# First stage of a two-layer attention and convolution trunk: layer 1's modulation columns computed with the modulation weights as stationary fp32 operand

## The chip, the cores and the metric

The kernel runs on one core of a Trainium2 chip. The metric is device time of one execution in microseconds (us); the time before is the median of three runs. A core has a matrix engine (PE, with its weight loads shown as PEld), a vector engine (DVE), a scalar engine (ACT), GpSimd (POOL), and a sync engine (SP) whose queue issues nearly all transfers. Each engine works through its own instruction queue in order and waits there on semaphores of the others.

## The reference

A trunk of two layers on 1024 latent tokens of width 1024 with 256 context tokens: layer 1 is windowed attention that also reads the context, layer 2 a convolution module. Only what feeds layer 1's input projection matters here:

```
silu_c = jax.nn.silu(c)
silu_cc = jax.nn.silu(c_ctx)
...
shift, scale, gate = jnp.split((silu_c @ ada_w[i] + ada_b[i])[:, None, :], 3, axis=-1)
h_lat = modulate(rmsnorm(x, norm_g[i]), shift, scale)
...
shift_c, scale_c, gate_c = jnp.split(silu_cc @ ada_w[i] + ada_b[i], 3, axis=-1)
h_ctx = modulate(rmsnorm(h_ctx_stream, norm_g[i]), shift_c, scale_c)
```

`modulate(h, shift, scale)` is `h * (1 + scale) + shift`. So for layer 1 two vectors (the condition c and the context's c_ctx, 1024 numbers each) are multiplied with the first 2048 columns of `ada_w[0]` (1024 x 3072, fp32; 8 MB of it are read here), and the results scale and shift the 1024 features of the normalised tokens, which are then multiplied with `attn_w_in`.

## The kernel before

Features lie on the 128 partitions, so the 1024 features are 8 tiles, numbered kt. Large products are in a three-term form: each fp32 operand is split into a high part (hh, whi: rounded to the fast fp32r format) and a low part (hl, wlo: the rest), and `mm3` multiplies whi with hh, whi with hl and wlo with hh. An fp32r matmul is one record in the trace.

**The first stage** (lines 310 to 548) makes the modulated, transposed tiles of x and multiplies them with the first three 128-column chunks of `attn_w_in` (key head 0, query head 0, value head 0), accumulated over kt in PSUM as `acc0`. Latent tokens are treated in two halves of 512: half 0 in this stage, half 1 in the loop from line 1071 on, after the results of half 0 (`finished0`) and the context's keys (`ctx0`).

- `ada_load(pr)` (280): loads for a pair of tiles (256 columns of shift and 256 of scale) four pages `araw` of 0.5 MB, each by two transfers with runs of 1 KB, and two short rows of `ada_b`.
- `ada_split` (386): splits each page into `ahi` (ACT) and `alo` (DVE).
- `ada_mm` (397): 16 fp32r matmuls per pair. The condition is the stationary operand, four columns (`c4`: high and low part of two vectors); 512 modulation columns are moving. The result is four rows in PSUM, copied to `R` (trace name arow).
- `ada_cols` (413): turns the rows into columns and adds high, low and bias parts: four fp32 matmuls per pair with the 5-row page of `R` as stationary operand and `sel` (two columns) moving. DVE then writes the shift and the gain, (1 + scale) times the norm weight, to `mods`.
- `sums`, `rstd_of`, `normalise` (339 to 360): row sums of squares, their reciprocal roots, scaling of the token rows. `sums` on ACT is a square (trace name junk) and a short accumulator read.
- `turn` (426): four PE transposes of the row pages give one tile with 512 tokens in PSUM. `x_tile` (432) and `modulated` (371): ACT writes hh from PSUM with gain and shift, DVE writes the full-precision value hf, then DVE or POOL writes hl = hf - hh. `c_tile` (442) does it for the context's 256 tokens.
- `x_mm` (453): three products for each listed weight chunk.
- `wsA.load` and `wsA.split` (212, 221): loads a chunk of `attn_w_in` (0.5 MB, runs of 512 bytes) and splits it on ACT and DVE.
- `spin` (306): products of zeros that nothing reads, placed between waits.

**Order.** A framework schedules instructions that are not pinned by a modelled time; `pin` names the engines whose instructions stay in program order from there on (P, V, A, G, S). PE and DVE are pinned throughout the stage, ACT only up to `pin("PV")` (504); SP is never pinned. Instructions of an unpinned engine can be moved ahead of pinned ones. In the loop over pairs (508) the next pair's `ada_mm` stands ahead of this pair's products, and tiles 0 and 1 of half 1 are turned in its last round (524, 536). All instructions are issued through one helper, so the trace gives the same line, L89, for all of them, and groups are told apart by tile names.

## Time and profile before

| | us |
|---|---|
| median of 3 runs (1755.21 to 1758.65) | 1755.38 |
| span of the profiled execution, first to last instruction | 1752.9 |
| PE busy | 1720.7 (98%) |
| PE weight loads busy | 1424.8 (81%) |
| DVE busy | 1148.3 (66%) |
| ACT busy | 889.4 (51%) |
| POOL busy | 895.4 (51%) |
| share of PE in the chain of work that ended last | 86% |

The mean granted PE clock over the span is 0.996. Records of PE overlap, since matmuls are pipelined: a lone duration is longer than the distance from one start to the next, and it is the distance that counts in a row of them. In the timeline a row is: start, duration, engine, line, operation, out<-in, shape, count, and in brackets how long the engine was idle before and what released it. In groups the two numbers behind the bar are total busy time and mean duration in nanoseconds.

### The profile page before, as it was taken

To read this page: it belongs to the slowest core of one execution; us is meant where nothing else is said; L and a number is where in the kernel's file an instruction comes from. 1 tells how busy PE (TensorE), PEld (TensorE's weight loads), DVE (VectorE), ACT (ScalarE), POOL (GpSimd) and SP (SyncE) were. 2 spreads that over 40 slices of the span, in tenths; PEclk is the share of its full clock that TensorE was granted. 3 is DMA by queue.
4 is the path that set the end of the run, shared out by engine and by line. 5 is a ranking of instruction groups with operands and counts; after the bars stand their busy time and mean duration, and the time that the engine had idled before them with its cause. 6 is when DMAs were issued, how large, how long until landed. Compare 5 with 4: busy or idle time off the path is not lost.

```text
span 1752.9 us, 23877 instructions
## 1 busy us (share of the span) xinstructions
PE 1720.7 (98%) x8420; PEld 1424.8 (81%) x8420; DVE 1148.3 (66%) x2079; ACT 889.4 (51%) x1548; POOL 895.4 (51%) x705
## 2 busy tenths in 40 slices
PE   7999999999999999999999999999999999999997
PEld 4788888888888888888888888888888888788886
DVE  6755564556546563656315189999999999867823
ACT  7555553445345444545334355554665564466731
POOL 0245654566636565653101267998898888130300
PEclk9999999999999999999999999999999999999999
DMA  9334443444334542436777733011121202377971
GB/s 313 107 82 139 136 133 85 145 147 145 100 105 143 152 142 87 136 119 203 279 250 239 241 90 105 13 54 31 43 79 36 91 30 79 120 254 243 325 264 48
DMA packets 195324, 242.45 MB, mean 138 GB/s; under 512 B 11798, under 2 KB 126790, under 8 KB 195204
## 3 DMA queue, kind: packets, MB, share of 16 engines
q1 hardware_dynamic: 188516, 230.10, 40.3%
q10 hardware_dynamic: 6688, 10.83, 2.6%
q8 instruction: 66, 1.08, 0.3%
q14 instruction: 54, 0.44, 0.1%
HBM read 188.70 MB, written 41.69 MB: 131 GB/s over the span
## 4 chain that ended last, share of the span: by engine, by line
PE 86%; DMA 5%; DVE 3%; POOL 2%; ACT 2%; issue 2%; SPq 1%; ACTq 0%; POOLq 0%; DVEq 0%
PE psg L89 44%; PE pss L89 22%; PE pso L89 19%; DMA araw_page<-in_ada_w_dram 1%; POOL rope_half L89 1%; DMA low_page<-in_conv_w_out_dram 1%; DMA rope_half<-rope_half 1%; SPq L89 1%; DMA low_page<-in_attn_w_out_dram 1%; DMA wolC<-low_page 1%; DVE mask_page L89 1%; ACT p_page L89 0%; POOL wlo_page L89 0%; POOL low_page L89 0%; DMA wraw_page<-in_attn_w_in_dram 0%
## 5 line engine op out<-in xcount | busy, mean ns | idle before, releaser
L89 POOL TENSOR_TENSOR odd_half<-odd_half,prod_half 128x513 f32<-128x513 f32 (+2 forms) x252 | 312.8, 1250 | 24.2 <-ACT prod_half L89 11.0
L89 PE MATMUL psg<-hh_page,whi_page 128*128 128x512 f32 x600 | 237.6, 396 | 0.0
L89 PE MATMUL psg<-hh_page,wlo_page 128*128 128x512 f32 x600 | 236.9, 395 | 0.0
L89 PE MATMUL psg<-hl_page,whi_page 128*128 128x512 f32 x600 | 236.8, 395 | 0.0
L89 POOL TENSOR_TENSOR wlo_page<-wraw_page,whi_page 128x1024 fp32r<-128x1024 f32 x70 | 173.1, 2475 | 104.1 <-ACT whi_page L89 83.2
L89 ACT ACTIVATE prod_half<-ubuf,dww 128x513 f32<-128x513 f32 (+2 forms) x252 | 165.1, 674 | 107.3 <-POOL odd_half L89 105.1
L89 POOL TENSOR_SCALAR p_page<-p_page,sc 128x640 f32<-128x640 f32 (+1 forms) x128 | 100.8, 787 | 224.4 <-DVE sc L89 208.7
L89 PE MATMUL psg<-h2h_page,whi_page 128*128 128x512 f32 x464 | 183.9, 396 | 0.0
L89 PE MATMUL psg<-h2h_page,wlo_page 128*128 128x512 f32 x464 | 183.0, 394 | 0.0
L89 PE MATMUL psg<-h2l_page,whi_page 128*128 128x512 f32 x464 | 182.4, 393 | 0.0
L89 DVE SCALAR_TENSOR_TENSOR pss<-ubuf,dww,pss 128x512 f32<-128x512 f32 (+3 forms) x270 | 172.3, 670 | 0.1
L89 DVE SCALAR_TENSOR_TENSOR pss<-ubuf,wsum,pss 128x512 f32<-128x512 f32 (+3 forms) x270 | 171.7, 670 | 0.2
L89 DVE TENSOR_TENSOR ptlo<-pss,pthi 128x640 fp32r<-128x640 f32 (+1 forms) x144 | 103.3, 717 | 64.0 <-ACT pthi L89 62.8
L89 ACT ACTIVATE p_page<-p_page,sc 128x641 f32<-128x641 f32 (+1 forms) x128 | 102.7, 802 | 74.1 <-DVE sc L89 69.7
L89 ACT ACTIVATE pthi<-pss 128x640 fp32r<-128x640 f32 (+1 forms) x144 | 88.6, 615 | 91.7 <-PE pss L89 86.3
L89 PEld LDWEIGHTS psg<-hh_page,wlo_page 128*128 128x128 f32 x600 | 112.9, 188 | 26.3
L89 PEld LDWEIGHTS psg<-hh_page,whi_page 128*128 128x128 f32 x600 | 113.0, 188 | 20.8 <-DVE kvc_page L89 0.2
L89 PEld LDWEIGHTS psg<-hl_page,whi_page 128*128 128x128 f32 x600 | 112.9, 188 | 20.7
L89 ACT ACTIVATE whi_page<-wraw_page 128x1024 fp32r<-128x1024 f32 x88 | 92.6, 1053 | 69.0 <-PE psg L89 25.5
L89 PE MATMUL pso<-h2l_page,whi_page 128*128 128x512 f32 x304 | 119.9, 394 | 0.0
L89 PE MATMUL pso<-h2h_page,whi_page 128*128 128x512 f32 x304 | 119.8, 394 | 0.0
L89 PE MATMUL pso<-h2h_page,wlo_page 128*128 128x512 f32 x304 | 119.6, 394 | 0.0
(244 smaller groups left out, 4105.2 us busy)
## 6 DMA issues: line engine op xcount, KB each, us to landing
wraw_page<-in_conv_w_in_dram SPq DMA_DIRECT2D x48, 512.0 KB
wraw_page<-in_attn_w_in_dram SPq DMA_DIRECT2D x40, 512.0 KB
wol_page<-wolA SPq DMA_DIRECT2D x32, 512.0 KB
wo_page<-in_attn_w_out_dram SPq DMA_DIRECT2D x32, 512.0 KB
wo_page<-in_conv_w_out_dram SPq DMA_DIRECT2D x32, 512.0 KB
wol_page<-wolC SPq DMA_DIRECT2D x32, 512.0 KB
rope_half<-rope_half ACTq DMA_DIRECT2D x80, 128.0 KB
araw_page<-in_ada_w_dram SPq DMA_DIRECT2D x32, 256.0 KB
```

The costliest lines, as they stand in the source:

```text
L89: r = f(*a, **k)
```

## The change

The modulation weights become the stationary operand. For tile kt and j (0 shift, 1 scale) `ada(kt)` multiplies eight 128x128 fp32 blocks of `ada_w`, unsplit, with two moving columns, the fp32 condition `c2`; the result is columns on the partitions at once. Bias and norm weight come in as per-partition scalars: the first 2048 elements of `ada_b` are loaded as 16 more rows of `crow` and transposed with it into `ab0`. `ada_split`, `ada_mm`, `ada_cols`, `c4`, `cf`, `R` and `sel` go.

Loads are per tile: `ada_load(kt)` brings two pages of 0.5 MB with runs of 512 bytes (tiles 0 to 3); `ada_load(4, 2)` and `ada_load(6, 2)` bring two tiles in four pages with runs of 1 KB. The first rows of x are now loaded ahead of all modulation weights, the context's rows after tile 5's weights.

The order of work is rewritten: for tiles 0, 1 and 2 `ada`, `turn`, `x_tile`, the split of one chunk, spins (30, 3, 3, 4 and 5 of them) and the products that are possible; then a loop in which each round has one `ada`, one `x_tile` and the products of the tile before. Context tiles are made two in a round from round 5 on. Tiles 0 and 1 of half 1 are turned after `ctx0("k", 0)`. The sums of squares of x's first half are shared by ACT and DVE, and all low parts of half 0 are made on DVE.

```diff
-ADA_FP = ()
 FILL = 12
+SPIN0 = 30
+SPIN1 = 3
 DEFER = 6
...
     vt = ctile([P, P], F32, "vt")
-    sel = ctile([P, 2], F32, "sel")
+    ab0 = ctile([P, 16], F32, "ab0")
     sink = ctile([P, NH], F32, "sink")
...
     crow_pg = hp.alloc(F32, None, "crow")
-    crow = crow_pg[0:32, 0:P]
+    crow = crow_pg[0:48, 0:P]
     SY.dma_start(out=crow[0:8], in_=c.rearrange("o (r p) -> (o r) p", p=P))
...
     SY.dma_start(out=crow[16:32], in_=norm_g.rearrange("l (r p) -> (l r) p", p=P))
+    SY.dma_start(out=crow[32:48], in_=ada_b[0:1, 0:2048].rearrange("o (r p) -> (o r) p", p=P))
     G.memset(ones, 1.0)
...
-    NPR = KT // 2
-    R = {}
     araw = {}
-    def ada_load(pr):
-        R[pr] = hp.alloc(F32, None, "arow")
-        araw[pr] = [pg.alloc(F32, [2, 2, 256], "araw") for _ in range(4)]
-        for i in range(4):
-            for j in range(2):
-                SY.dma_start(out=araw[pr][i][:, :, j],
-                             in_=ada_w[0, i * 256:i * 256 + 256, j * D + pr * 256:j * D + pr * 256 + 256]
+    def ada_load(kt, n=1):
+        w = n * P
+        for j in range(2):
+            for i in range(n):
+                t = pg.alloc(F32, [KT // n, w], "araw")
+                for m in range(n):
+                    araw[(kt + m, j)] = araw.get((kt + m, j), []) + [(t, slice(m * P, m * P + P))]
+                SY.dma_start(out=t, in_=ada_w[0, i * D // n:(i + 1) * D // n, j * D + kt * P:j * D + kt * P + w]
                              .rearrange("(k p) n -> p k n", p=P))
-        for j in range(2):
-            SY.dma_start(out=R[pr][4:5, j * 256:j * 256 + 256], in_=ada_b[0:1, j * D + pr * 256:j * D + pr * 256 + 256])
...
     spin(4)
+    xs0 = load_rows(x[0, 0:512], 4)
     ada_load(0)
-    xs0 = load_rows(x[0, 0:512], 4)
     wsA.load()
...
     wsA.load()
+    ada_load(2)
     wsA.load()
-    ada_load(2)
...
     tp = ps_g()
-    PE.transpose(tp[:, 0:32], crow, ident[0:32, 0:32])
+    PE.transpose(tp[:, 0:48], crow, ident[0:48, 0:48])
     act(cs, tp[:, 0:16], AF.Silu)
     V.tensor_copy(vt[:, 96:112], tp[:, 16:32])
+    V.tensor_copy(ab0[:, 0:8], tp[:, 32:40])
+    V.tensor_scalar(out=ab0[:, 8:16], in0=tp[:, 40:48], scalar1=1.0, scalar2=None, op0=ALU.add)
     hp.free(crow_pg)
-    ada_load(3)
-    cx = load_rows(ctx[0], 2)
     act(small([P, 1], name="warm", bufs=1), cs[:, 0:1], AF.Sqrt, scale=0.0)
...
     hp.free(zer_pg)
-    c4 = ctile([P, KT, 4], F32R, "c4")
-    csv = cs.rearrange("p (r k) -> p k r", r=2)
-    V.tensor_copy(c4[:, :, 0:2], csv)
-    tt(V, c4[:, :, 2:4], csv, c4[:, :, 0:2].bitcast(F32), ALU.subtract)
+    c2 = ctile([P, KT, 2], F32, "c2")
+    V.tensor_copy(c2, cs.rearrange("p (r k) -> p k r", r=2))
...
-    mods = [ctile([P, 4, 2], F32, f"mod{pr}") for pr in range(NPR)]
+    mods = [ctile([P, 2, 2], F32, f"mod{kt}") for kt in range(KT)]
...
     Hc = []
-    cf = ctile([P, KT, 4], F32, "cf")
-    G.memset(cf[:, :, 2:4], 0.0)
-    V.tensor_copy(cf[:, :, 0:2], csv)
...
-    def ada_split(pr, which=range(4)):
-        for i in which:
-            if (pr, i) not in ADA_FP:
-                raw = araw[pr][i]
-                rv = raw.rearrange("p a b c -> p a (b c)")
-                h, l = pg.alloc(F32R, [2, 512], "ahi"), pg.alloc(F32R, [2, 512], "alo")
-                act(h, rv, AF.Copy)
-                split_lo(V, l, rv, h)
-                pg.free(raw)
-                araw[pr][i] = (h, l)
-    def ada_mm(pr):
-        o = ps_o(0)
-        for i in range(4):
-            for k in range(2):
-                if (pr, i) in ADA_FP:
-                    r = araw[pr][i].rearrange("p a b c -> p a (b c)")
-                    parts = [(cf, r)]
-                else:
-                    parts = [(c4, r) for r in araw[pr][i]]
-                for n, (c, r) in enumerate(parts):
-                    PE.matmul(o[0:4], c[:, 2 * i + k, :], r[:, k], start=i + k + n == 0,
-                              stop=i + k == 4 and n == len(parts) - 1)
-            pg.free(*(araw[pr][i] if len(parts) == 2 else (araw[pr][i],)))
-        V.tensor_copy(R[pr][0:4, 0:512], o[0:4])
-    def ada_cols(pr):
-        rw, m = R.pop(pr), mods[pr]
-        cps = ps_o(1)
-        for i in range(4):
-            PE.matmul(cps[:, 2 * i:2 * i + 2], rw[0:5, i * P:(i + 1) * P], sel[0:5], start=True, stop=True)
-        hp.free(rw)
+    def ada(kt):
+        o, m = ps_o(0), mods[kt]
+        for j in range(2):
+            for i, (t, sl) in enumerate(araw[(kt, j)]):
+                nk = t.shape[1]
+                for k in range(nk):
+                    kk = i * nk + k
+                    PE.matmul(o[:, 2 * j:2 * j + 2], t[:, k, sl], c2[:, kk], start=kk == 0, stop=kk == KT - 1)
+        for j in range(2):
+            for t, _ in araw.pop((kt, j)):
+                if not any(t is u for v in araw.values() for u, _ in v):
+                    pg.free(t)
         with tc.high_priority():
-            V.tensor_copy(m[:, 0:2], cps[:, 0:4].rearrange("p (a b) -> p a b", b=2))
-            for i in range(2):
-                V.tensor_scalar(out=m[:, 2 + i], in0=cps[:, 4 + 2 * i:6 + 2 * i], scalar1=1.0,
-                                scalar2=vt[:, 96 + 2 * pr + i:97 + 2 * pr + i], op0=ALU.add, op1=ALU.mult)
+            V.tensor_scalar(out=m[:, 1], in0=o[:, 2:4], scalar1=ab0[:, 8 + kt:9 + kt],
+                            scalar2=vt[:, 96 + kt:97 + kt], op0=ALU.add, op1=ALU.mult)
+            V.tensor_scalar(out=m[:, 0], in0=o[:, 0:2], scalar1=ab0[:, kt:kt + 1], scalar2=None, op0=ALU.add)
...
         sl = slice(half * 512, half * 512 + 512)
-        m, i = mods[kt // 2], kt % 2
+        m = mods[kt]
         with tc.high_priority():
-            modulated(tp, [(Hh[kt][:, sl], Hl[kt][:, sl], lambda f: f[:, 0:512])], m[:, 2 + i, 0:1], m[:, i, 0:1], 512, eng, True)
+            modulated(tp, [(Hh[kt][:, sl], Hl[kt][:, sl], lambda f: f[:, 0:512])], m[:, 1, 0:1], m[:, 0, 0:1], 512, eng, True)
...
-        m, i = mods[kt // 2], kt % 2
+        m = mods[kt]
         if kt % 4 == 0:
...
         modulated(turn(cx, kt, lambda: ps_o(bank))[:, 0:CT], [(h, l, lambda f: f[:, 0:CT])],
-                  m[:, 2 + i, 1:2], m[:, i, 1:2], CT, V, "A")
+                  m[:, 1, 1:2], m[:, 0, 1:2], CT, V, "A")
         if kt == KT - 1:
...
     pin("PVA")
-    ada_split(0)
-    spin(10)
-    ss0 = sums(xs0, (A, A, A, A))
-    ada_mm(0)
-    ada_cols(0)
-    spin(18)
+    spin(SPIN0)
+    ss0 = sums(xs0, (A, V, A, V))
     r0 = rstd_of(ss0, D, 4)
-    wsA.split(lambda: scale_rows(xs0, r0, (V, V, A, A)))
+    ada(0)
+    scale_rows(xs0, r0, (V, A, V, A))
+    x_tile(turn(xs0, 0, ps_g), 0, 0, V)
+    wsA.split()
+    spin(SPIN1)
+    sa, sb = ps_s(), ps_s()
+    acc0 = [sa[:, 0:512], sa[:, 512:1024], sb[:, 0:512]]
+    ada_load(3)
+    ada_load(4, 2)
+    cx = load_rows(ctx[0], 2)
+    ctodo = deque(range(KT))
+    x_mm(0, 0, acc0, (0,))
+    spin(3)
+    ada(1)
+    x_tile(turn(xs0, 1, ps_g), 1, 0, V)
+    wsA.split()
+    spin(4)
+    ada_load(6, 2)
     xs1 = load_rows(x[0, 512:1024], 4)
-    tps = [turn(xs0, kt, ps_g) for kt in range(2)]
-    sa, sb = ps_s(), ps_s()
-    acc0 = [t[:, i * 512:i * 512 + 512] for t in (sa, sb) for i in range(2)]
-    ctodo = deque(range(KT))
+    x_mm(1, 0, acc0, (0,))
+    x_mm(0, 0, acc0, (1,))
+    x_mm(1, 0, acc0, (1,))
+    ada(2)
+    x_tile(turn(xs0, 2, ps_g), 2, 0, V)
+    wsA.split()
+    vec_pages = load_vecs()
+    spin(5)
+    x_mm(2, 0, acc0, (0, 1))
     for kt in range(2):
-        x_tile(tps[kt], kt, 0, V)
-    spin(5)
+        x_mm(kt, 0, acc0, (2,))
     pg.free(zer_r)
-    x_mm(0, 0, acc0, (0,))
-    x_mm(1, 0, acc0, (0,))
     pin("PV")
-    ada_split(1)
-    wsA.split()
-    wsA.split()
-    for pr in range(NPR):
-        a, b = 2 * pr, 2 * pr + 1
-        which = range(3) if pr else (1, 2)
-        if pr + 1 < NPR:
-            ada_mm(pr + 1)
-        if pr + 2 < NPR:
-            ada_split(pr + 2, (0, 1))
-        if pr == 2:
-            normalise(xs1, ss1, (G, G, A, G))
-        x_mm(a, 0, acc0, which)
-        if pr + 1 < NPR:
-            tp = turn(xs0, a + 2, ps_g)
-            ada_cols(pr + 1)
-            x_tile(tp, a + 2, 0, V)
-        else:
-            turn_vecs(*vec_pages)
-            x_tile(turn(xs1, 0, ps_g), 0, 1, V)
-        if pr + 2 < NPR:
-            ada_split(pr + 2, (2, 3))
-        if pr == 1:
-            ssc = sums(cx, (A, A))
-        if pr > 1:
-            c_tile(ctodo.popleft(), 0)
-            c_tile(ctodo.popleft(), 1)
-        x_mm(b, 0, acc0, which)
-        if pr + 1 < NPR:
-            x_tile(turn(xs0, b + 2, ps_g), b + 2, 0, G)
-        else:
-            x_tile(turn(xs1, 1, ps_g), 1, 1, V)
-        if pr > 1:
-            c_tile(ctodo.popleft(), 0)
-            c_tile(ctodo.popleft(), 1)
-        if pr == 1:
-            normalise(cx, ssc, (G, A))
-            vec_pages = load_vecs()
-            ss1 = sums(xs1, (A, A, A, A))
-        if pr == 2:
-            pg.free(*xs0)
-            cos, sin = (pg.alloc(F32, [1024], n) for n in ("cos", "sin"))
-            SY.dma_start(out=cos, in_=k_cos)
-            SY.dma_start(out=sin, in_=k_sin)
+    x_mm(2, 0, acc0, (2,))
+    for kt in range(3, KT + 1):
+        if kt < KT:
+            ada(kt)
+            x_tile(turn(xs0, kt, ps_g), kt, 0, V)
+        if kt == 4:
+            normalise(cx, sums(cx, (A, A)), (V, A))
+        if kt == KT:
+            normalise(xs1, sums(xs1, (A, A, A, A)), (V, G, A, V))
+        for n in range(3 if kt > 3 else 0):
+            x_mm(kt - 1, 0, acc0, (n,))
+            if n < 2 and kt >= 5:
+                c_tile(ctodo.popleft(), n)
+    pg.free(*xs0)
+    cos, sin = (pg.alloc(F32, [1024], n) for n in ("cos", "sin"))
+    SY.dma_start(out=cos, in_=k_cos)
+    SY.dma_start(out=sin, in_=k_sin)
+    turn_vecs(*vec_pages)
...
     ctx0("k", 0)
+    for kt in range(2):
+        x_tile(turn(xs1, kt, lambda: ps_o(kt)), kt, 1, V)
     sa = ps_s()
```

More of the change, by code (lines that the diff above doesn't have):

```diff
@@ L99, in backbone_kernel @@
     conv_w_in, conv_b_in, conv_dw_w, conv_dw_b, conv_ln_g, conv_ln_b, conv_w_out, final_g,
-    k_cos, k_sin, k_mask, k_ident, k_sel,
+    k_cos, k_sin, k_mask, k_ident,
     out,
@@ L296, in load_rows @@
         return ts
-    SY.dma_start(out=sel, in_=k_sel)
     zer_pg = hp.alloc(F32, None, "zer")
@@ L1698, in _constants @@
     k_mask = np.concatenate([prev, z, nxt, z, z], 1)
-    sel = np.zeros((P, 2), f)
-    sel[[0, 2, 4], 0] = 1
-    sel[[1, 3, 4], 1] = 1
-    return {"k_cos": k_cos, "k_sin": k_sin, "k_mask": k_mask, "k_ident": np.eye(P, dtype=f), "k_sel": sel}
+    return {"k_cos": k_cos, "k_sin": k_sin, "k_mask": k_mask, "k_ident": np.eye(P, dtype=f)}
 _INS = ["x", "c", "ctx", "c_ctx", "ada_w", "ada_b", "norm_g", "attn_w_in", "attn_sink", "attn_w_out",
```

## The prediction

> **What bounds the kernel now.** I read the page's busy shares first (TensorE 98% of the span), then the table of windows cut at the stage's own milestones.

> ```profile
> 0.00:25.00 25.00, 18.11 (x71) 10.99 (x71) 11.03 (x27) 17.75 (x24) 0.92 (x7) 1.00 0.90 291
> 25.00:50.00 25.00, 21.53 (x88) 11.98 (x88) 20.32 (x24) 19.72 (x25) 1.28 (x1) 0.86 1.02 330
> 50.00:77.30 27.30, 25.90 (x144) 19.66 (x145) 21.18 (x50) 16.25 (x32) 8.16 (x7) 1.00 0.32 96
> 77.30:101.46 24.16, 21.35 (x116) 17.27 (x115) 14.18 (x17) 9.24 (x15) 4.89 (x4) 1.00 0.20 54
> 101.46:1752.90 1651.44, 1633.85 (x8007) 1364.88 (x8005) 1081.64 (x1962) 826.47 (x1454) 880.14 (x687) 1.00 0.42 135
> ```

> Columns: stretch, its length, busy time of PE, PEld, DVE, ACT, POOL, granted clock, DMA share, GB/s. From 101.46 on PE is busy 1633.85 of 1651.44 us, and the built instruction order there is the same in both kernels on every queue. So whatever the change does to the moment at which PE gets there stays to the end: the question is only the first 101 us. Up to 50 us the transfers are the limit (share 0.90 and 1.02); from 50 us on they are not (0.32), and there PE is.

> The timeline says when bytes arrive, from ACT instructions that a DMA released:

> ```profile
> 17.47 1.06 ACT L89 ACTIVATE junk_page<-x_page 128x1024 f32<-128x1024 f32 x1 [0.18 <-DMA x_page<-in_x_dram]
> 19.24 1.06 ACT L89 ACTIVATE whi_page<-wraw_page 128x1024 fp32r<-128x1024 f32 x1 [0.18 <-DMA wraw_page<-in_attn_w_in_dram]
> 30.48 1.06 ACT L89 ACTIVATE ahi_page<-araw_page 128x1024 fp32r<-128x1024 f32 x1 [0.53 <-DMA araw_page<-in_ada_w_dram]
> 31.98 1.06 ACT L89 ACTIVATE ahi_page<-araw_page 128x1024 fp32r<-128x1024 f32 x1 [0.45 <-DMA araw_page<-in_ada_w_dram]
> 42.81 1.06 ACT L89 ACTIVATE junk_page<-x_page 128x1024 f32<-128x1024 f32 x1 [0.20 <-DMA x_page<-in_ctx_dram]
> 44.08 1.06 ACT L89 ACTIVATE junk_page<-x_page 128x1024 f32<-128x1024 f32 x1
> ```

> 4 MB (modulation pair 0, then x) are there at 17.3. A modulation page of 0.5 MB in 1 KB runs costs 1.50 us (30.48 to 31.98), a chunk of `attn_w_in` in 512-byte runs 1.77 (17.47 to 19.24). The first context page is there at 42.6, behind 11.5 MB.

> **The clock.** The same table at the stretches around the only two in which the clock was halved:

> ```profile
> 23.39:26.80 3.41, 1.71 (x7) 1.00 1.19 302
> 26.80:30.21 3.41, 3.41 (x8) 0.50 1.12 333
> 40.45:43.87 3.42, 1.21 (x6) 1.00 1.01 354
> 43.87:47.28 3.41, 3.41 (x10) 0.50 1.01 394
> 57.52:60.93 3.41, 2.99 (x22) 1.00 0.29 118
> 60.93:64.35 3.42, 3.35 (x20) 1.00 0.02 5
> ```

> Here PE alone is shown. A stretch of 3.41 us with 1.71 or 1.21 us of PE work was followed by one at 0.50; 57.52 to 60.93, much of whose work was transposes and the two-column fp32 products of `ada_cols`, was not.

> **The change part by part.** Price of the new operation, an fp32 stationary 128x128 with two columns moving:

> ```profile
> 16.40 1.05 PE L89 MATMUL pso<-sel,arow_half 5*128 5x2 f32 x8 [0.77 <-DVE arow_half L89]
> L89 PE MATMUL pso<-sel,arow_half 5*128 5x2 f32 x32 | 4.2, 249 | 0.8 <-DVE arow_half L89 0.8
> 328.03 0.53 PEld L89 LDWEIGHTS pso<-ones,mask_page 128*128 128x128 f32 x4
> L89 PEld LDWEIGHTS pso<-ones,mask_page 128*128 128x128 f32 x32 | 4.2, 192 | 0.0
> 30.96 0.40 PE L89 MATMUL pso<-ahi_page,c 128*4 128x512 f32 x1
> 31.19 0.40 PE L89 MATMUL pso<-alo_page,c 128*4 128x512 f32 x1
> ```

> `ada_cols` has 16 products in the program and 32 records: each fp32 product is two passes. Eight passes took 1.05 us with the last lasting 0.25, so they start (1.05-0.25)/7 = 0.114 apart; with 128 rows loaded, four loads in 0.53 us, the last 0.19: (0.53-0.19)/3 = 0.113. The new `ada` has 16 products for a tile, 32 passes, **3.6 us**; eight tiles, 28.8 us of PE. Removed are 64 fp32r products 0.23 apart (30.96 to 31.19), 14.7 us, and 32 passes of `ada_cols`, 3.6 us. PE gets 10.5 us more work. No row shows many such passes in a train; as bounds I take half a pass (0.057) and the whole 0.19 us of one load, which both rows contradict; the value is 0.113, where two different rows meet.

> Removed and added elsewhere, from the groups of the first 77.3 us:

> ```profile
> L89 ACT ACTIVATE ahi_page<-araw_page 128x1024 fp32r<-128x1024 f32 x16 | 16.6, 1053 | 7.3 <-DMA araw_page<-in_ada_w_dram 7.2
> L89 DVE TENSOR_TENSOR alo_page<-araw_page,ahi_page 128x1024 fp32r<-128x1024 f32 x16 | 18.9, 1217 | 4.9 <-ACT ahi_page L89 4.9
> L89 DVE COPY arow_half<-pso 4x512 f32<-4x512 f32 x4 | 2.7, 675 | 1.8 <-PE pso L89 1.8
> L89 ACT ACTIVATE junk_page<-x_page 128x1024 f32<-128x1024 f32 x10 | 10.6, 1056 | 1.3 <-ACT junk_page L89 0.4 <-DMA x_page<-in_ctx_dram 0.2 <-DMA x_page<-in_x_dram 0.2
> L89 ACT ACTIVATE hh_page<-psg,mod 128x512 fp32r<-128x512 f32 x10 | 7.5, 769 | 4.2 <-DVE abt L89 2.1 <-PE psg L89 1.5 <-DVE mod L89 0.5
> L89 DVE TENSOR_SCALAR hf_page<-psg,mod 128x512 f32<-128x512 f32 x10 | 8.1, 808 | 8.7 <-ACT hh_page L89 8.7
> L89 DVE TENSOR_TENSOR hl_page<-hf_page,hh_page 128x512 fp32r<-128x512 f32 x7 | 4.8, 692 | 0.2
> L89 ACT ACTIVATE whi_page<-wraw_page 128x1024 fp32r<-128x1024 f32 x3 | 3.2, 1054 | 0.6 <-DMA wraw_page<-in_attn_w_in_dram 0.6
> L89 DVE TENSOR_TENSOR wlo_page<-wraw_page,whi_page 128x1024 fp32r<-128x1024 f32 x3 | 3.6, 1225 | 0.0
> ```

> The splits go: 16.6 us of ACT, 18.9 + 2.7 of DVE. They were beside transfers for the most part (ACT waited 7.2 us for DMA), so I credit them nothing by themselves; what they give is an earlier start, worked out now. A tile's chain from transposes to usable low part is 0.77 (hh) + 0.81 (hf) + 0.69 (hl), about 2.35 us with hand-overs; a chunk's low part another 1.22 behind it on DVE.

> Tile 0: x and two pages of 512-byte runs are 3 MB, 2 x 1.5 us less than the 4 MB at 17.3 plus 2 x 0.27 for the runs: 14.8. The second half of `ada(0)` ends at 16.5. DVE's two row scalings now stand behind the modulation columns in its order, so the transposes end at about 18.6; chain and low chunk give the third product at 22.6 (now 26.98, row below): **4.4 us gained**. Tile 1: 3 spins and `ada(1)` to 27, transposes 27.4, chain and chunk 31.0, four products more: 32.0. Tile 2: `ada(2)` to 35.6, transposes 36.0. Here a wait comes in: in ACT's built order the two squares of the context (`sums(cx)`) stand ahead of tile 2's hh. Ahead of the context page are 9.5 MB instead of 11.5, 4 x 1.5 us less than 42.6, but eight pages more have 512-byte runs, 8 x 0.27: 38.8; the second 1.3 later; two squares of 1.06 and their 0.19 reads end at 41.4. Queued behind them are hh, the third chunk's split and so all 15 products of tile 2's turn, and PE in program order behind those. hh 42.2, hl 43.7, chunk low 44.9, products until 46.5; PE idle from 37 brings a halved stretch, 1 us: PE reaches `ada(3)` at **47.5**.

> From there PE has what it needs: five tiles of `ada` 18.0, 45 products of `x_mm` at 0.23 10.4, nine fours of transposes (five tiles, four of context) at 0.4 3.6, and 1.0 where the four squares of x's second half (4 x 1.25 on ACT) stand ahead of tile 7's hh. The last product of half 0 ends at 47.5 + 33.0 = 80.5.

> ```profile
> 26.98 0.63 PE L89 MATMUL pss<-hh_page,wlo_page 128*128 128x512 f32 x1
> 70.29 0.40 PE L89 MATMUL pss<-hh_page,wlo_page 128*128 128x512 f32 x1
> 70.53 0.60 PE L89 MATMUL psg<-ident,x_page 128*128 128x128 f32 x4
> 74.87 0.40 PE L89 MATMUL pss<-hh_page,whi_page 128*128 128x512 f32 x1
> 77.31 0.48 PE L89 MATMUL pss<-hh_page,whi_page 128*128 128x512 f32 x1
> 68.18 0.61 DVE L89 SCALAR_TENSOR_TENSOR mask_page<-ident,abt,mask_page 128x128 f32<-128x128 f32 x2
> 74.45 0.68 DVE L89 TENSOR_TENSOR rope_page<-pss,cos_page 128x512 f32<-128x512 f32 x1
> ```

> Now it ends at 70.53: **10.0 us lost**. Half 1's first products follow now after 4.34 us (74.87), its second tile starts at 77.31. In the change tiles 0 and 1 of half 1 are turned only behind the context's products, and their hf stands on DVE behind two rope products of 0.68, mask work of 0.61 and copies. PE is ready 4.5 us after the last product, hl about 8 after it. That costs 3.5 us, between 1.5 (only the chain of 2.35, less what PE does meanwhile) and 4.5; half 1 has then less ACT and DVE work in arrears, for which I give back 0.5. Sum: 10.0 + 3.0 = **13.0 us slower**, a profiled span of 1765.9. The median lies 2.5 above the span (1755.38 against 1752.9): **1768.4**, with 1763 to 1774 its own range. SP's issue order changes, but its queue has no new wait until the cosine table, whose page comes free only at the end of half 0 (about 75) and which is wanted at 80; its 512 KB take 1.3 us. The longer crow load, the small copies and `ab0` lie under the 30 spins, which end near 12 and so before the first modulation page; without that cover they cost 0.5. Removing POOL's hl work costs or gives nothing, the chain uses DVE.

> **Rivals.** (a) *The two-column passes don't hold the clock.* In a step of 6.5 us (3.6 `ada`, 0.4 + 0.4 transposes, 2.1 products) a stretch of 3.41 us would have on average 1.5 us of counted work, under the 1.71 that was followed by 0.50. Half of the stretches halved turns 33 us into 44, and the first three tiles lose 3: 1768.4 + 14 = 1782. For it: two halved stretches already, from gaps. Against: 57.52 to 60.93. [...]

> (b) *The context's squares don't hold tile 2.* If the context comes earlier than 38.8 by some 5 us, PE reaches `ada(3)` at 42.5: 1763. Against: transfers arrive in the order of issue, and 9.5 MB (10.0 million bytes) at the stage's 291 to 330 GB/s take 30 to 34 us from about 4.5 on.

> (c) *A pass in a train is much cheaper than 0.113.* Place: the 240 passes on PE's path (all but the first half of `ada(0)`). At half, 0.057, they give back 13.4 us and the change is at 1755; at 0.04 it is 4.5 us faster, 1751. It decides at 0.059 a pass. For it: a load of 4 columns lasts less than half as long and nothing shows a long train; against: 5 and 128 rows gave the same 0.114 and 0.113, in trains of eight and four. That PE's earlier start is carried through is no rival by itself: 28.8 + 16.7 + 12 us (transposes, context, spins) of PE work behind 14.8 cannot end before 72, where half 1 starts now at 74.87, and each tile's chain comes on top.

> **How the numbers follow.** Forecast 0.55, (a) 0.20, (b) 0.10, (c) 0.15. Likeliest 1768. The range reaches to (a) and to the better half of (c), 1753 to 1784; loads of 0.19 each without overlap (240 x 0.077 = 18.5 more, 1787) are left out with (c)'s tail. A measurement tells about 0.2% (3.5 us) from no change: (c) is split into 0.09 faster and 0.06 same; with 0.01 from (b) that is 0.09, 0.07, 0.84.

> **What would show it.** `pso<-c,araw_page` with 256 records starting 0.113 apart; the two context squares just ahead of tile 2's hh, released by DMA near 39; `ada(3)` at 47 to 48; the last product of half 0 near 80; half 1's second tile near 90; a PE-bound run from 101 us on with the same length as now. The clock column at 0.50 in several stretches between 47 and 80 would mean (a); starts of passes 0.06 apart (c).

## The result and the profile after

| | before | after |
|---|---|---|
| median of 20 runs, us (range) | 1755.61 (1752.54 to 1758.65) | 1763.05 (1753.59 to 1767.77) |
| span of the profiled execution, us | 1752.9 | 1754.5 (its time 1756.26) |
| mean granted clock of the profiled execution | 0.996 | 0.985 |
| PE busy, us | 1720.7 | 1725.0 |

The change makes the kernel 0.37% slower: ratio 1.0037, interval 1.0029 to 1.0045. The runs of after spread over 14 us, those of before over 6, and the profiled execution of after is the second fastest of its 20, so its trace shows less loss than the median has.

The table of windows, cut where that of before was cut (stretch, length, busy time of PE, PEld, DVE, ACT, POOL, granted clock, DMA share, GB/s):

```profile
0.00:25.00 25.00, 20.54 (x82) 15.20 (x83) 9.21 (x26) 9.26 (x13) 0.88 (x6) 0.85 0.90 286
25.00:50.00 25.00, 24.61 (x128) 21.39 (x129) 6.08 (x10) 5.75 (x8) 0.00 (x0) 0.74 0.94 340
50.00:77.30 27.30, 27.30 (x146) 25.28 (x146) 8.62 (x23) 5.86 (x10) 0.00 (x0) 0.65 0.01 2
77.30:101.46 24.16, 21.81 (x132) 18.01 (x131) 15.96 (x37) 15.94 (x31) 4.20 (x3) 0.97 0.36 112
101.46:1754.50 1653.04, 1630.71 (x8111) 1380.38 (x8109) 1094.89 (x1978) 834.49 (x1467) 884.13 (x689) 1.00 0.42 136
```

DVE and ACT have lost their work of the first 77 us, as the change meant. PE is busy without a gap from 50.00 to 77.30, but at a granted clock of 0.65, where before had 1.00. The milestones on PE:

```profile
22.88 0.80 PE L90 MATMUL pss<-hh_page,wlo_page 128*128 128x512 f32 x1 [0.34 <-DVE wlo_page L90]
...
47.42 0.95 PE L90 MATMUL pso<-c,araw_page 128*128 128x2 f32 x8
...
89.37 0.40 PE L90 MATMUL pss<-hh_page,wlo_page 128*128 128x512 f32 x1
```

Before, the third product started at 26.98 and the last of half 0 at 70.29. It now starts at 89.37, 19.1 us later. The tail behind it:

```profile
95.15 0.49 PE L90 MATMUL pss<-hh_page,whi_page 128*128 128x512 f32 x1 [0.43 <-ACT hh_page L90]
96.95 0.50 PE L90 MATMUL pss<-hl_page,whi_page 128*128 128x512 f32 x1 [1.30 <-DVE hl_page L90]
...
99.28 0.48 PE L90 MATMUL pss<-hh_page,whi_page 128*128 128x512 f32 x1
```

Half 1's second tile starts at 99.28 against 77.31: 22.0 us late. Yet the span is only 1.6 us longer. So there are two things to explain: where 22 us went in the stage, and where 20 came from behind it.

**The stage: the clock.** PE alone, in stretches of 3.41 us. The trace of after changes the granted clock at 17.28, 34.35, 41.18, 44.59 us and so on, each time a whole number of 3.413 us behind the first, so the clock is one value in each stretch:

```profile
48.00:51.42 3.42, 3.42 (x32) 1.00 0.14 42
51.42:54.83 3.41, 3.41 (x18) 0.50 0.00 0
54.83:58.24 3.41, 3.41 (x18) 0.50 0.00 0
58.24:61.66 3.42, 3.42 (x12) 0.50 0.00 0
61.66:65.07 3.41, 3.41 (x29) 1.00 0.01 2
65.07:68.48 3.41, 3.41 (x16) 0.50 0.00 0
...
78.72:82.14 3.42, 3.42 (x27) 1.00 0.00 0
82.14:85.55 3.41, 3.41 (x27) 1.00 0.01 2
```

Each stretch is shown as fully busy, and still some are followed by 0.50. What tells them apart is what PE was busy with. Counted in the trace by start (a product here is an fp32r matmul with 512 moving columns, a pass one of the two records of an fp32 product of `ada`):

```
stretch        512-column products  transposes  two-column passes   clock of the next
48.00:51.42            0                4              26             0.50
61.66:65.07            3                0              25             0.50
78.72:82.14            5                2              18             1.00
82.14:85.55            5                6              14             1.00
```

In all, 44 us of the stage and its surroundings ran at half clock (12 stretches in the stage, one at 396 us, the ramps at both ends of the kernel left out), against 7 before.

**Behind the stage: the products.** PE alone between 1300 and 1500 us, in which both kernels do the same work; first before, then after:

```profile
1300.00:1500.00 200.00, 198.51 (x857) 1.00 0.18 57
```

```profile
1300.00:1500.00 200.00, 200.00 (x884) 1.00 0.18 58
```

27 more records fit into the same 200 us, at the same granted clock. From 1100 to 1500 us the starts of neighbouring 512-column products are 223 to 242 ns apart in before (mean 231.4, three longer or shorter ones left out), and 226 or 227 in after, without one exception among 1764 distances. I call the one uneven, the other even. Neither the chain of waits nor the clock column shows it; it came out only when the start times of the two identical instruction streams were laid side by side from the end: after was 20.3 us late at 75 us, 22.0 at 77, 15 at 1060, 5 at 1560 and 1.6 at the end. Added up over the aligned streams from 77 us on, 5658 distances of neighbouring products gave after 24.9 us; all else, waits and the halved stretch at 396 us, took 4.5 of it back. So the products alone account for the 20.4.

### The profile page after: what moved, and what is told of

Same layout as the page of the kernel before. It is cut to its first block, busy times and chain, and to the rows that moved or that the text cites. A ratio compares the mean times of both kernels' runs of the same rounds, so it can differ in the third digit from the quotient of the medians.

```text
span 1754.5 us, 24127 instructions
## 1 busy us (share of the span) xinstructions
PE 1725.0 (98%) x8592; PEld 1460.3 (83%) x8592; DVE 1134.8 (65%) x2073; ACT 871.3 (50%) x1528; POOL 889.2 (51%) x698
## 4 chain that ended last, share of the span: by engine, by line
PE 88%; DMA 4%; DVE 3%; POOL 2%; ACT 2%; issue 1%; SPq 0%; ACTq 0%; POOLq 0%; DVEq 0%
PE psg L90 44%; PE pss L90 23%; PE pso L90 21%; DMA rope_half<-rope_half 1%; POOL rope_half L90 1%; DMA low_page<-in_conv_w_out_dram 1%; POOL wlo_page L90 1%; DMA x_page<-in_x_dram 0%; DVE mask_page L90 0%; DMA wo_page<-in_conv_w_out_dram 0%; DMA wraw_page<-in_attn_w_in_dram 0%; DVE p_page L90 0%; ACT p_page L90 0%; DMA ozf_page<-ozd 0%; DVE hf_page L90 0%
## 5 line engine op out<-in xcount | busy, mean ns | idle before, releaser
L90 POOL TENSOR_TENSOR odd_half<-odd_half,prod_half 128x513 f32<-128x513 f32 (+2 forms) x252 | 313.4, 1251 | 23.8 <-ACT prod_half L90 10.6
L90 PEld LDWEIGHTS psg<-hl_page,whi_page 128*128 128x128 f32 x600 | 112.9, 188 | 18.5
```

Of the source, the lines that this page charges most:

```text
L90: r = f(*a, **k)
```

## The experiments

The theory for the stage was the clock, with PE work and waiting chains as the rival. For the even products the first theory was the addresses of the pages, since the change of the constants' sizes moved all pages from 32 above a multiple of 64 bytes to a multiple of 64.

### Addresses: e1, e2

In both kernels, among the constants:

```diff
+    pad = ctile([P, 8], F32, "pad")
+    G.memset(pad, 0.0)
```

> The kernel before with one more tile of 32 bytes per partition among its constants (a memset on POOL fills it, nothing reads it), so that every tile behind it, all pages and pthi/ptlo included, moves up by 32 bytes and starts at a multiple of 64 bytes, as in the changed kernel, instead of 32 above one. No other instruction differs. Theory (addresses): the 512-column products' starts were 0.2315 us apart before and 0.2267 after because of where the pages start; then this kernel has 0.2267 too and runs about 22 us faster than the kernel before, 1734 us (1728 to 1740). Rival (the rate belongs to the new order of work or to the chip of that run): same time, 1753 to 1758, with 0.2315.

> The changed kernel with the same 32 bytes added, so that its pages start 32 bytes above a multiple of 64, as in the kernel before. This shows the change without its side effect on addresses. Theory (addresses): the distance of products goes up to 0.2315 us and the time to about 1784 us (1778 to 1790), some 28 us above the kernel before: all that is lost in the first stage stays to the end. Rival: no change, 1760 to 1766.

Measured: e1 1755.29 us, ratio to before 0.9991 (0.9981 to 1.0001); e2 1764.31, ratio 1.0043 (1.0022 to 1.0064). PE alone from 1300 to 1500 us, e1 and then e2:

```profile
1300.00:1500.00 200.00, 198.51 (x856) 1.00 0.18 57
```

```profile
1300.00:1500.00 200.00, 200.00 (x884) 1.00 0.19 59
```

e1 stays uneven and e2 even: the addresses are not it, and the theory falls. e2 has the same stage as after, and in its profiled execution the last product of half 0 starts at 94.43 instead of 89.37, with 51 us at half clock instead of 41.

### Holding the clock by products between the passes: e3

```diff
+    def zero_mm(into):
+        PE.matmul(into, zer_r[:, 0:P], zer_r[:, 0:512], start=True, stop=True)
...
-    ada(1)
+    ada(1, [[zb] * 4] * 2)
...
-            ada(kt)
+            ada(kt, ([zb] * 4, x_parts(kt - 1, 0, acc0, range(3)) if kt > 3 else [zb] * 4))
```

> The changed kernel with 512-column products between the two-column ones: in ada(0) to ada(2) a product of zeros after every second of the 16, in ada(3) to ada(7) one product that nothing reads after every second of the first eight (after all in ada(3)), and the previous tile's nine products spread over the last eight. 48 products of 0.23 us more, of which 24 stand where PE waits for transfers; 24 x 0.23 = 5.5 us more PE work in line. Theory (clock): the clock stays at 1.00 through most of the stage, the ~41 us at 0.50 go, and the last product of half 0 ends near 79 instead of 89.6: 1763 - 16 + 5.5 = 1752 (1748 to 1757). Rival (the lost 20 us are PE work and waiting chains, the clock only fills waits): 1763 + 5.5 = 1768 or more.

Measured: 1786.17 us, ratio 1.0152 (1.0113 to 1.0190). Neither reading said that. PE alone:

```profile
53.43:56.85 3.42, 3.42 (x15) 1.00 0.02 5
56.85:60.26 3.41, 3.41 (x27) 1.00 0.00 0
60.26:63.67 3.41, 3.41 (x15) 0.50 0.00 0
63.67:67.09 3.42, 3.42 (x16) 0.50 0.00 0
67.09:70.50 3.41, 3.41 (x15) 0.50 0.00 0
```

From 56.85 to 60.26 there are 5 products and 20 passes, and then the clock is at 0.50 for 47.8 us in a piece. This even mixture made the slowest kernel of all: a stretch of e3 with 5 products beside 20 passes was followed by 0.50 each of the three times, and the stretches at half clock behind 60.26 held only 1 to 5 products, and the clock stayed at 0.50 through them. What I expected of the interleaving was wrong. The added work does not explain the loss (24 products of 0.23 us in line would be 5.5 us, and 23 were lost against after); the 47.8 us at half clock do.

### Holding the clock by wider passes: e5, e9

```diff
-    c2 = ctile([P, KT, 2], F32, "c2")
-    V.tensor_copy(c2, cs.rearrange("p (r k) -> p k r", r=2))
+    c2 = ctile([P, 2 * KT + NC], F32, "c2")
+    G.memset(c2[:, 2 * KT:2 * KT + NC], 0.0)
+    V.tensor_copy(c2[:, 0:2 * KT].rearrange("p (k r) -> p k r", r=2), cs.rearrange("p (r k) -> p k r", r=2))
...
-    PE.matmul(o[:, 2 * j:2 * j + 2], t[:, k, sl], c2[:, kk], start=kk == 0, stop=kk == KT - 1)
+    PE.matmul(o[:, NC * j:NC * j + NC], t[:, k, sl], c2[:, 2 * kk:2 * kk + NC], start=kk == 0, stop=kk == KT - 1)
```

NC is 256 in e5 and 128 in e9; only the first two columns of each result are used.

> The changed kernel with 256 moving columns instead of 2 in ada: the two of the condition and the 254 that follow them in a tile that ends in zeros; the results of the other 254 are not read. Number, order and waits of the instructions stay. The trace of the changed kernel has fp32 passes of 256 columns (the context's) 0.117 to 0.120 us apart against 0.112 for two columns, so PE gets 256 x 0.007 = 1.8 us more work. Theory (the clock): a window full of such passes streams over 7000 columns and is not followed by 0.50; the ~41 us at half clock go nearly all, which gives back 16 to 18 us: 1763 - 15 = 1748 (1743 to 1752). Rival (the loss of the stage is PE work and chains): 1763 to 1767, whatever the clock does.

> As with 256 moving columns, but 128: by the run with 256, where a pass took 0.2150 to 0.219 us (0.84 ns a column), 128 columns stream in 0.108 us, under the 0.112 that a two-column pass takes anyway, so PE gets nothing to do that is longer. Theory (the clock cost the stage 16 to 18 us, and columns that stream are what holds it): the clock stays at 1.00 nearly everywhere, the last product of half 0 ends near 75 instead of 89.6, and the time is 1763 - 16 = 1747 (1743 to 1751), below both kernels. Rival (the clock follows something else, or the held clock is paid back later): 1755 or more.

Measured: e5 1770.44 us, ratio 1.0086 (1.0071 to 1.0101); e9 1745.19 us, ratio **0.9939** (0.9923 to 0.9955), below both kernels. The groups of passes in after, e5 and e9 (x256; busy time, mean ns of one):

```profile
L90 PE MATMUL pso<-c,araw_page 128*128 128x2 f32 x256 | 36.8, 279 | 0.3 <-DVE ms L90 0.3
```

```profile
L91 PE MATMUL pso<-c,araw_page 128*128 128x256 f32 x256 | 57.2, 381 | 0.1
```

```profile
L91 PE MATMUL pso<-c,araw_page 128*128 128x128 f32 x256 | 31.7, 285 | 0.2
```

e5 held the clock (it shows one stretch at 0.50 in the stage) and still lost, because my price was wrong: I took the context's 256-column products, which are fp32r, for fp32 passes. An fp32 pass of 256 columns takes 0.216 us in e5 (the starts are 0.215 to 0.219 apart), not 0.119, so PE got 256 x 0.104 = 27 us more. That number gave 0.108 for 128 columns, less than the 0.112 that a pass takes anyway, and e9 shows that they cost nothing: the passes of e9 start 111 or 112 ns apart, those of after the same at full clock. PE alone in e9, in the stretches that answer to those of after above:

```profile
48.63:52.04 3.41, 3.30 (x30) 1.00 0.14 43
52.04:55.45 3.41, 3.41 (x24) 1.00 0.00 0
55.45:58.87 3.42, 3.42 (x33) 1.00 0.01 2
58.87:62.28 3.41, 3.41 (x24) 1.00 0.00 0
62.28:65.69 3.41, 3.41 (x33) 1.00 0.02 5
```

PE has the same instructions in the same order, the passes 126 idle columns wider, and here the clock stays. It is not held everywhere: around the stage e9 has three halved stretches left, against 12 in after:

```profile
21.32:24.73 3.41, 2.95 (x7) 0.50 1.14 344
24.73:28.14 3.41, 3.41 (x18) 0.50 1.10 343
86.17:89.58 3.41, 3.41 (x11) 0.50 0.56 159
```

e9's last product of half 0 starts at 77.78 (expected to end near 75), half 1 at 83.58 (after 95.15, before 74.87), and its second tile at 89.10 (after 99.28, before 77.31):

```profile
77.78 0.40 PE L91 MATMUL pss<-hh_page,wlo_page 128*128 128x512 f32 x1
83.58 0.49 PE L91 MATMUL pss<-hh_page,whi_page 128*128 128x512 f32 x1 [0.76 <-ACT hh_page L91]
89.10 0.70 PE L91 MATMUL pss<-hh_page,whi_page 128*128 128x512 f32 x1
```

So the part of the clock that the wider passes win back is 1763.05 - 1745.19 = 17.9 us of the median, and with it won back the stage is 8.7 us late at half 1's first product and 11.8 at its second tile. Of these 11.8 some 1.3 are the stretch from 86.17 on: five products start 0.43 us apart there instead of 0.23, and four transposes take 0.70 instead of 0.36.

### The tail: e4

```diff
     turn_vecs(*vec_pages)
+    for kt in range(2):
+        x_tile(turn(xs1, kt, ps_g), kt, 1, V)
...
     ctx0("k", 0)
-    for kt in range(2):
-        x_tile(turn(xs1, kt, lambda: ps_o(kt)), kt, 1, V)
```

> The changed kernel with tiles 0 and 1 of half 1 turned at the end of half 0, behind turn_vecs, instead of behind the context's key products. Theory (chain in the open, as predicted at 3.5 us): 2.5 to 4 us faster than the changed kernel, about 1760. Rival (ACT and DVE are in arrears at that point, so the place of the turn does not matter): within 1 us of 1763.

Measured: 1762.11 us, ratio to before 1.0035 (1.0022 to 1.0048), 0.9 us under after. The number alone is the rival's. But its profiled execution spent 55 us at half clock in the stage and its tail, after's 41, so a gain of 3 us cannot be told from it. What its trace does show is that the wait is gone: PE starts half 1 at 104.02 and goes through its first tile and into the second without idling, where after waits 0.43 us for hh and 1.30 for hl. What that is worth stays open; the tail is read in after and e9, below.

### What makes the products even: e6, e7, e8, e10, e11, e12

Each of these takes one thing of the old way of making columns out of before, or puts it into after. e6 (before, wide stationary), e7 and e8 (after, some of its 30 first spins replaced):

```diff
-    c4 = ctile([P, KT, 4], F32R, "c4")
+    c4 = pg.alloc(F32R, [KT, P], "c4")
+    for i in range(2):
+        V.tensor_copy(c4[:, 4 * i:4 * i + 4], zer.rearrange("p (k c) -> p k c", c=P))
```

```diff
+        PE.matmul(idle[0:4], zer_r[:, 0:4], zer_r[:, 0:512], start=True, stop=True)
```

```diff
+        PE.matmul(idle[:, 2 * i:2 * i + 2], ones[0:5], ones[0:5, 0:2], start=True, stop=True)
```

> The kernel before with the condition's four stationary columns widened to 128 by zeros (one page more in the stage), so that no fp32r product with a 4-column stationary operand is left. Theory (small operand): the uneven distance of 0.2315 us between products comes from these products; without them it is 0.2267 and the kernel some 22 us faster, 1734 us. Rival (something else makes the products uneven, or the programs differ in it as a whole): 0.2315 and 1753 to 1758.

> The changed kernel with 16 of its 30 first spins made with a 4-column stationary operand of zeros (fp32r), as the kernel before has them in ada_mm; nothing reads the result. Theory (small operand): the products from 102 us on become uneven, 0.2315 us apart, and the time goes to about 1785. Rival: 0.2267 as in the changed kernel, 1754 to 1768.

> The changed kernel with 16 of its 30 first spins replaced by fp32 products with 5 rows and two moving columns, as the kernel before has them in ada_cols; nothing reads the result. Theory (few rows): the products from 102 us on become uneven, 0.2315 us apart, about 1785. Rival: 0.2267 as in the changed kernel, 1754 to 1768.

Measured: e6 1755.22 us (ratio 0.9999, 0.9989 to 1.0008) and uneven; e7 1755.71 and e8 1762.21 in single runs, both even. Neither the 4-column nor the 5-row operand makes products uneven where it is added, and taking the 4-column one out does not make them even.

e10 puts the new `ada` into the old order: `ada(0)`, `ada(1)` for `ada_mm(0)` and `ada_cols(0)`, and in the loop:

```diff
-            ada_mm(pr + 1)
+            ada(a + 2)
+            ada(b + 2)
```

> The new ada alone: the stage of the kernel before, with its order of loads and of work (pairs of tiles, POOL's share, half 1's first tiles at the end of half 0), but ada(2pr), ada(2pr+1) at the place of ada_mm(pr), modulation pages not split, bias and norm weight as in the changed kernel. Two readings. What makes the products uneven in the kernel before: if the split products with 4 columns, the 5-row products, or the short transfers that feed them, the distance goes to 0.2267; if the order of work or POOL's part in it, it stays 0.2315. The time: PE gets 10.5 us more work in the stage and some 10 us of half clock from two-column passes, so 1755 + 20 = 1776 with uneven products and 1754 with even ones.

Measured: 1757.01 us, ratio 1.0003 (0.9992 to 1.0015), with even products:

```profile
1300.00:1500.00 200.00, 200.00 (x884) 1.00 0.19 58
```

Its last product of half 0 starts at 95.54, 25 us later than in before, after 55 us at half clock; the even products bring nearly all of it back. So none of the order of work, the loads of x ahead, POOL's share and the place of half 1's first tiles is needed to make the products even; the way in which the columns are made is, or something that changes with it.

e11 (128 rows instead of 5, `sel` made on DVE) and e12 (all small things out at once):

```diff
-            PE.matmul(cps[:, 2 * i:2 * i + 2], rw[0:5, i * P:(i + 1) * P], sel[0:5], start=True, stop=True)
+            PE.matmul(cps[:, 2 * i:2 * i + 2], rw[:, i * P:(i + 1) * P], sel, start=True, stop=True)
```

> The kernel before with two things taken out of its way of making columns: the 5-row stationary operand of ada_cols becomes one of 128 rows (the page's other rows set to zero on POOL), and sel, whose transfer moves 8 bytes a row, is made on DVE from the identity matrix instead of being loaded. What is left of the difference to the run with the new ada alone is the 4-column products, the splits of the modulation pages, the four-row copies and the bias rows' transfers. If the uneven distance of products comes from the 5-row operand or the 8-byte transfer, it goes to 0.2267 us and the time to 1755 - 22 = 1733 (1728 to 1738), the fastest of all; if it comes from what is left, it stays 0.2315 and 1753 to 1758.

> The kernel before without anything small in the way it makes columns: 128-column and 128-row stationary operands throughout (zeros beyond the four columns), sel made on DVE, copies of the product rows over all 128 partitions, no transfers of bias rows (the bias comes in by crow's 48 rows and as per-partition scalars, as in the changed kernel). What is left of the difference to the run with the new ada alone is the splitting of the modulation pages, the shape of their transfers and the fp32r products with the condition stationary. If one of the small things makes the products uneven, whichever of them, their distance goes to 0.2267 us and the time to about 1734 (1729 to 1739); if not, it stays at 0.2315 and 1753 to 1758, and the cause lies in what is left or in the program as a whole.

Measured: e11 1755.03 us, ratio 0.9999 (0.9987 to 1.0010); e12 1758.03, ratio 1.0004 (0.9994 to 1.0013); both uneven. e12:

```profile
1300.00:1500.00 200.00, 199.95 (x864) 1.00 0.18 56
```

What is left: the splitting of the modulation pages on ACT and DVE, the shape of their transfers, the fp32r products with the condition stationary, or the program as a whole. Of the last kind one number goes along with it in all fourteen traces: the instruction transfers of the larger queue are 66 packets in the five uneven kernels, 67 or 68 in the nine even ones. That is a coincidence until someone varies it alone; it was not tried. The cause stays open.

## Why the prediction was right, and where it was not

Forecast 1768 us (1753 to 1784, slower 0.84), measured 1763.05. Sign and range held. The sum without the clock came out near its forecast, but the total did so by luck: two effects that the sum left out, one of 17.9 us and one of some 21 the other way, nearly cancelled.

**The price of the pass was right.** 0.113 was forecast from two short trains; in the long one, at full clock, 32 passes take 3.70 us, and their starts are 0.111 or 0.112 apart:

```profile
13.09 3.70 PE L90 MATMUL pso<-c,araw_page 128*128 128x2 f32 x32 [0.34 <-DVE ms L90]
```

Rival (c), a much cheaper pass, is out. Crediting the removed splits with nothing but an earlier start held too: ACT and DVE have less to do, and the third product starts at 22.88 (forecast 22.6).

**The wait of tile 2 was not there.** The context's squares were to hold hh until 41.4:

```profile
35.32 1.06 ACT L90 ACTIVATE junk_page<-x_page 128x1024 f32<-128x1024 f32 x1 [1.03 <-DMA x_page<-in_ctx_dram]
...
36.62 1.06 ACT L90 ACTIVATE junk_page<-x_page 128x1024 f32<-128x1024 f32 x1
...
41.30 0.78 ACT L90 ACTIVATE hh_page<-psg,mod 128x512 fp32r<-128x512 f32 x1 [3.53 <-PE psg L90]
```

The context landed at 35.3, not 38.8, and the squares were done at 37.8. The arrival was the term mis-sized: the prediction's other reckoning, from 291 to 330 GB/s, gave 34.5 to 38.5, and it took the late end (from 25 to 50 us after moved 340). hh did start at 41.30, but it waited 3.53 us for PE, which had done `ada(1)` at half clock (6.7 us from 24.75 on instead of 3.6). `ada(3)` at 47.42, forecast 47.5, is therefore a coincidence, not a confirmation; with the clock held it starts at 45.10 in e9. That is rival (b)'s premise, with half the gain that it priced.

**The failed step of the stage: the clock.** The forecast let the two-column passes hold it, with rival (a) at 0.20 and +14 us. The runs show rival (a): +17.9 us, e9 against after. My evidence for the other side was the stretch of before from 57.52 to 60.93: I put its clock down to the two-column passes and left its transposes out of account. No run shows that such passes hold the clock, and the traces decide against that reading: that stretch had 4 products and 8 transposes beside 8 passes of two columns and was followed by 1.00, while all 60 stretches of the fourteen traces (up to 105 us) that had at most 4 products, beside two-column passes or nothing, and no transpose were followed by 0.50.

**The sum without the clock was near.** 10.0 us were forecast for the end of half 0 and 3.0 for the tail with its give-back, 13.0 together. From `ada(3)` to the end of half 0 the forecast was 33.0 us; e9 needs 32.9 (from 45.10 to 0.24 behind the start of the last product at 77.78). Its stage is 7.5 us late (77.78 against 70.29), and the 2.5 that the forecast had too much are the wait of tile 2 that was not there. The tail costs 2.9 us in after (9.91 from the last product of half 0 to half 1's second tile, 7.02 before), where DVE's hl keeps PE waiting 1.30, and 4.3 in e9, 1.3 of them the halved stretch at 86.17: about the 3.0 of the forecast both times.

**The failed step behind the stage: "whatever the change does to the moment at which PE gets there stays to the end".** The instruction order from 101.46 on is the same in both, but its pace is not. e9's lag goes from 11.8 us to 9.8 us ahead at the end (1743.1 against 1752.9), 21.6 us gained; in after the distances of products alone gave 24.9. That a stream of identical instructions has one duration was taken for granted and had no rival.

The terms together: 1755.6 + 11.8 (stage and tail) + 17.9 (clock) - 21.6 (behind the stage) = 1763.7, measured 1763.05. This is bookkeeping and no test, since the last three are read from e9 and its distance to before and after. Without the even products the change would have been at 1785 or so, just outside the range; without either effect at 1767.

## What to carry to other kernels

Here stretches full of passes with two moving columns had PE busy for 3.41 of 3.41 us and were still followed by a clock of 0.50. Widening the moving operand with columns that nobody reads, up to the time that a pass takes anyway (here 128 columns of fp32, 0.112 us), was free and worth 18 us (1745.19 against 1763.05), while spreading 512-column products evenly among such passes made it worse (e3, 1786.17). So where the clock column drops under a busy PE, count what streams in each stretch. And before a shift at one place is carried to the end of a kernel, lay the two instruction streams side by side from the end: if the lag changes where nothing was edited, the change has a side effect that no wait shows.

## What the runs showed of the hardware that was not expected

**The pass.** An fp32 pass with a 128x128 stationary operand starts 0.112 us after the one before, with 2 columns (after) as with 128 (e9); with 256 (e5) it is 0.216. At half clock the two-column passes of after start 0.213 apart, so they, too, were slower at the lower clock.

**Even and uneven products.** Fourteen profiled kernels, the same products behind the stage, and two paces: from 1100 to 1500 us 226.7 ns in the nine with the new `ada`, nearly all 226 or 227, and about 231.4, from 223 to 242, in the five without. From 105 to 900 us the nine are less even (224 to 239 for nearly all, mean 228.2 in after) but still faster than the five (mean 232.1 in before). It is worth some 21 us of 1755, more than the whole change, and its cause is not known.
